# State-space mixer of a two-layer hybrid trunk: outputs formed by channel, two heads side by side in the array, and one scratch tag for two mixers' statistics

## The chip, the cores and the metric

The kernel runs on one core of a Trainium2 chip. Its engines are TensorE (PE, matrix products into PSUM; PEld is its weight load), VectorE (DVE), ScalarE (ACT), GpSimd (POOL) and SyncE (SP, which here issues DMAs). Each engine works through its own queue of instructions in order; semaphores make one wait for another. The metric is the device time of one execution in microseconds.

## The reference

Two layers, each with four token mixers (state-space SSD, RWKV-7, RG-LRU, retention) over one input projection and one output projection, and a SwiGLU feed-forward block behind them. 528 tokens (16 learned ones ahead of 512), width 1024. The mixer that the change rewrites is SSD, with 4 heads of 64 channels, 2 groups with a state of 128, in chunks of 128 tokens:

```python
def ssd_chunked(x, a, b, c):
    ...
    a_cs = jnp.cumsum(a, axis=-1)
    Lmat = jnp.exp(segsum(a))
    y_diag = jnp.einsum('bclhn,bcshn,bhcls,bcshp->bclhp', c, b, Lmat, x)
    decay_states = jnp.exp(a_cs[..., -1:] - a_cs)
    states = jnp.einsum('bclhn,bhcl,bclhp->bchpn', b, decay_states, x)
    ...
    entering = jnp.einsum('bhzc,bchpn->bzhpn', decay_chunk, states)[:, :-1]
    y_off = jnp.einsum('bclhn,bchpn,bhcl->bclhp', c, entering, jnp.exp(a_cs))
    return (y_diag + y_off).reshape(Bsz, T, H, P)
```

RWKV and retention end in a norm over each head's 64 channels, for which sums of squares by token and head are wanted (`head_group_norm`).

## The kernel before

Activations lie with channels on the partitions and tokens along the free axis, in two halves of 264 tokens. Every dense weight is streamed from DRAM as units of 128 output channels by 1024 inputs, 98 to a layer (24 of the input projection, 8 of the output projection, 44 and 22 of the feed-forward). ScalarE casts a unit to a high part and VectorE subtracts it to get the low part (L187, names `whi`, `wlo`). A unit times half the tokens is 8 k-tiles of three matmuls (L369 to L371, high by high, high by low, low by high). These are the projection matmuls. They write a PSUM bank of the pool `psb` (three banks, `pb`) or `psr` (three, `mr`); a third pool `psm` (two, `mx`) serves the mixers.

The mixers lie between the input projection and the output projection. RWKV's core (`rwkv_core`) goes through five packs p = 0 to 4, each two chunks of 64 tokens, pack 4 the tail of 16 tokens. A pack starts with transposes (L644), inverts a triangular matrix by substitution on VectorE (L675 to L684, a reduce, rounds of a shuffle with two tensor operations, and a transpose at the end), forms its results on TensorE (from L692 on, to the state's L769) and ends with `tok_stats`: ScalarE squares the pack's output into a scratch tile `gn_sq` (L448), VectorE sums it by head. Retention (`ret_core`) goes through five chunks c of 128 tokens (the last has 16) and ends each with a copy and the same `tok_stats`. SSD (`ssd_core`) goes through the same chunks; RG-LRU starts with the projection lx0, copied out of PSUM at L806.

The kernel is written in program order, in `layer`: RWKV's core and its end, then retention, then SSD's convolutions, dt and core, RG-LRU, the gates, and the ends. A scheduler then puts the instructions of all engines in an order of its own, by what they need. What bounds it are the slots of pools: a tile of a pool with k slots waits until the tile that had the slot k allocations earlier in program order is read for the last time. Two pools matter here. `up` has 16 slots of [128, 540], taken by projected tiles: retention's q, k, v and its rotation tables are among them, and hold their slots to the end of retention's chunks. `small` holds scratch tiles by tag; the scratch of `tok_stats` (L447) has one slot a tag. RWKV's calls use the tag `rw_sq` (L776), retention's `re_sq` (L1049).

In SSD's core a chunk forms `L`, the decay by pair of tokens times C·B (L887 to L894), and then token-major outputs: four matmuls with L as the weights and 64 columns each (L897), and from chunk 1 on two matmuls of C with the state, 128 columns each (L903). VectorE scales the second part by `ea`, exp of the decay's running sum, and adds the first into `ysb` (L905, L906). Two transposes turn `ysb` to channel-major (L921), and VectorE adds the skip term into `syf` (L922).

Of the kernel before, what the change touches and what calls it, by code (L numbers as in the profile page):

```python
# [14 lines left out]
ALU = mybir.AluOpType  # L15
# [29 lines left out]
# rows of the output projection, in the order in which y is held  # L45
Y_ORDER = ["rwkv0", "rwkv1", "lru0", "lru1", "ret0", "ret1", "ssd0", "ssd1"]

# [14 lines left out]
def constants():  # L62
    """Tables that depend on shapes alone."""
# [21 lines left out]
    # retention  # L85
# [26 lines left out]
def trunk(ctx, tc, hT, wstream, wdt, cols, lora, lruw, const, rope, out, dbg=None):  # L112
# [15 lines left out]
    # the identity is the first of the constants  # L128
# [13 lines left out]
    # ------------------------------------------------------------------ helpers  # L142
# [34 lines left out]
    def behind(after):  # L177
        """not to be issued ahead of the instructions given"""
        stack = ExitStack()
        for a in after:  # L180
            stack.enter_context(tc.issue_after(a.ins))
        return stack
# [6 lines left out]
    def rsqrt_small(v, n, m):  # L189
        """1/sqrt of [n, m], by Newton's steps."""  # L190
# [11 lines left out]
    def softplus_small(x, n, m):  # L202
        """log(1 + exp(x)) of [n, m]."""
# [17 lines left out]
    # ------------------------------------------------------------------ weights  # L221
    class Stream:
# [13 lines left out]
        def split(self, after=()):  # L236
            """after: instructions that it is not to be issued ahead of"""
# [26 lines left out]
    # ------------------------------------------------------------------ norms  # L264
    def rstd_bc(accs, n, keep=None, prior=None):
        """sums of squares, by partition in each of accs [128, n], -> 1/rms on every partition (in PSUM).
        keep: a place for 1/rms by token; prior: such a place, with factors that the squares still lack"""
# [25 lines left out]
    class SumSq:  # L293
        """squares of tiles, summed over the tiles"""
# [4 lines left out]
        def add(self, srcs):  # L299
            """the square of a pair of tiles"""  # L300
# [20 lines left out]
    def pair(name, n, where=None):  # L321
        """high and low part of [128, n], in one slot"""
# [12 lines left out]
    def norm_half(hs, n, wcol, ss, first=False):  # L335
        """8 tiles of h, in pairs [128, 2, n] -> the parts of rms_norm(h)"""
# [11 lines left out]
    def scaled_parts(t, n, wcol, k):  # L348
        """the parts of h * w, for one k-tile"""
# [8 lines left out]
    def load_h(src, s, n, engines=(nc.sync,), tile=pair_tile):  # L358
        """the 8 tiles of h, in pairs"""
# [5 lines left out]
    def big(ps, wt, acts, first, last):  # L365
        """ps += wt.T @ acts over the k-tiles listed"""
# [9 lines left out]
    def product(w, acts, n, i=0):  # L376
        """one unit of weights times 8 k-tiles of activations"""
# [4 lines left out]
    # ------------------------------------------------------------------ start  # L382
# [28 lines left out]
    # the table with the square root, for the squares too  # L411
# [4 lines left out]
    # derived parameters  # L416
# [957 lines left out]
```

## Time and profile before

| what | value |
|---|---|
| runs | 1520.08, 1522.01, 1521.93 us; median 1521.93 |
| the profiled execution, its span | 1520.8 us, 29707 instructions |
| TensorE busy | 1488.2 us (98%), 12654 instructions |
| VectorE busy | 805.9 us (53%) |
| ScalarE busy | 608.1 us (40%) |
| GpSimd busy | 6.0 us |
| DMA | 129.93 MB, mean 85 GB/s |

Engines overlap, so busy times don't add up to the span. A matmul's record runs from its start to a modelled end, and matmuls overlap in the array: distances between starts tell more than durations. An f32 matmul leaves two records, a transpose or a matmul of the split parts one. The granted clock (PEclk) is 1.00 at TensorE's full 2.4 GHz and 0.50 at 1.2 GHz.

### The profile page before, as it was taken

Reading aid. Unit: us, or ns where it says so; the run is one execution under the profiler, and the core shown is the slowest. Engines: PE = TensorE matmul, PEld = TensorE weight load, DVE = VectorE, ACT = ScalarE, POOL = GpSimd, SP = SyncE. Lnnn points to the kernel's source line nnn. Section 1 sums busy time; section 2 is a strip of 40 time slices with the busy share of each in tenths; the row PEclk is TensorE's granted clock in tenths of the full one; section 3 lists DMA queues with packets and bytes.
Section 4 is the critical chain, followed back from the end, with each engine's and each line's share of the span. In section 5 each row is a group of like instructions: output and inputs, shape, how many; then the busy total and the mean of one; then the engine's idle time right before and its main releaser. Section 6 shows DMA issues by size and latency. Waiting matters only on the chain.

```text
span 1520.8 us, 29707 instructions
## 1 busy us (share of the span) xinstructions
PE 1488.2 (98%) x12654; PEld 1432.1 (94%) x12654; DVE 805.9 (53%) x1961; ACT 608.1 (40%) x1132; POOL 6.0 (0%) x12
## 2 busy tenths in 40 slices
PE   7999999999999999999999999999999999999997
PEld 6998889999999999999999988899999999999997
DVE  7486656866534444322284866568665444443233
ACT  6633334756423332223255333348564233332231
POOL 0000000000000000000000000000000000000000
PEclk9999999999999999999999999999999999999998
DMA  7110100045212222222352101000551222322223
GB/s 243 64 57 29 43 29 29 29 157 166 70 56 84 84 98 97 84 93 88 112 197 63 57 29 42 29 29 30 154 179 56 70 98 85 110 84 98 98 91 104
DMA packets 50820, 129.93 MB, mean 85 GB/s; under 512 B 5120, under 2 KB 23680, under 8 KB 50560
## 3 DMA queue, kind: packets, MB, share of 16 engines
q1 hardware_dynamic: 47728, 124.22, 25.2%
q10 hardware_dynamic: 2960, 3.81, 0.8%
q8 instruction: 99, 1.62, 0.4%
q14 instruction: 33, 0.27, 0.1%
HBM read 119.50 MB, written 8.52 MB: 84 GB/s over the span
## 4 chain that ended last, share of the span: by engine, by line
PE 91%; DVE 5%; DMA 1%; ACT 1%; issue 1%; SPq 0%; DVEq 0%; ACTq 0%
PE pb L369 14%; PE pb L370 14%; PE pb L371 14%; PE mr L371 10%; PE mr L369 10%; PE mr L370 10%; PE mr L692 1%; PE mr L726 1%; PE mx L273 1%; DVE wlo L187 1%; PE mr L702 1%; PE mr L660 1%; DMA raw<-in_wstream_dram 1%; PE mr L766 1%; PE mr L756 1%
## 5 line engine op out<-in xcount | busy, mean ns | idle before, releaser
L369 PE MATMUL pb<-hn,whi 128*128 128x264 f32 (+1 forms) x1440 | 419.1, 291 | 2.4 <-ACT hn L187 2.4
L371 PE MATMUL pb<-hn,wlo 128*128 128x264 f32 (+1 forms) x1440 | 417.9, 290 | 0.0
L370 PE MATMUL pb<-hn,whi 128*128 128x264 f32 (+1 forms) x1440 | 416.5, 289 | 0.8 <-DVE hn L187 0.6
L187 DVE TENSOR_TENSOR wlo<-raw,whi 128x1024 fp32r<-128x1024 f32 x200 | 243.8, 1223 | 233.5 <-ACT whi L187 232.9
L187 ACT CAST whi<-raw 128x1024 fp32r<-128x1024 f32 x200 | 209.0, 1050 | 326.5 <-PE pb L370 131.6
L369 PEld LDWEIGHTS pb<-hn,whi 128*128 128x128 f32 x1440 | 272.7, 189 | 8.6 <-issue 3.4
L370 PEld LDWEIGHTS pb<-hn,whi 128*128 128x128 f32 x1440 | 273.3, 190 | 5.3 <-issue 2.0
L371 PEld LDWEIGHTS pb<-hn,wlo 128*128 128x128 f32 x1440 | 272.2, 189 | 3.3 <-issue 1.7
L369 PE MATMUL mr<-hn,whi 128*128 128x264 f32 (+1 forms) x800 | 228.3, 285 | 0.0
L371 PE MATMUL mr<-hn,wlo 128*128 128x264 f32 (+1 forms) x800 | 227.4, 284 | 0.1
L370 PE MATMUL mr<-hn,whi 128*128 128x264 f32 (+1 forms) x800 | 226.4, 283 | 0.0
L370 PEld LDWEIGHTS mr<-hn,whi 128*128 128x128 f32 x800 | 152.0, 190 | 0.0
L369 PEld LDWEIGHTS mr<-hn,whi 128*128 128x128 f32 x800 | 151.9, 190 | 0.0
L371 PEld LDWEIGHTS mr<-hn,wlo 128*128 128x128 f32 x800 | 150.9, 189 | 0.4 <-DVE wlo L187 0.4
L163 DVE TENSOR_TENSOR gf<-gf,mr 128x264 f32<-128x264 f32 (+1 forms) x88 | 37.4, 425 | 133.7 <-PE mr L371 130.0
L369 PE MATMUL mr<-g,whi 128*128 128x264 f32 (+1 forms) x352 | 99.9, 284 | 0.0
L370 PE MATMUL mr<-g,whi 128*128 128x264 f32 (+1 forms) x352 | 99.8, 284 | 0.0
L371 PE MATMUL mr<-g,wlo 128*128 128x264 f32 (+1 forms) x352 | 99.5, 283 | 0.0
L369 PE MATMUL pb<-g,whi 128*128 128x264 f32 (+1 forms) x352 | 99.4, 282 | 0.0
L370 PE MATMUL pb<-g,whi 128*128 128x264 f32 (+1 forms) x352 | 99.4, 282 | 0.0
L371 PE MATMUL pb<-g,wlo 128*128 128x264 f32 (+1 forms) x352 | 99.3, 282 | 0.0
L187 ACT CAST g<-gf 128x264 fp32r<-128x264 f32 (+1 forms) x88 | 35.9, 407 | 111.6 <-DVE gf L163 111.6
(397 smaller groups left out, 2406.0 us busy)
## 6 DMA issues: line engine op xcount, KB each, us to landing
raw<-in_wstream_dram SPq DMA_DIRECT2D x200, 512.0 KB, 3.5
h<-in_hT_dram SPq DMA_DIRECT2D x16, 264.0 KB, 4.5
hdram<-h SPq DMA_DIRECT2D x16, 264.0 KB, 3.0
h<-hdram SPq DMA_DIRECT2D x16, 256.0 KB, 3.9
h<-hdram SPq DMA_DIRECT2D x8, 264.0 KB, 5.3
hdram<-h SPq DMA_DIRECT2D x8, 256.0 KB, 2.2
cst<-in_const_dram SPq DMA_DIRECT2D x1, 1046.5 KB, 8.2
out_dram<-h SPq DMA_DIRECT2D x4, 256.0 KB, 2.6
```

The lines of the kernel that those rows point to most:

```text
L163: eng.tensor_tensor(out=out, in0=in0, in1=in1, op=op)
L187: last_hilo[:] = (S.copy(out=hi, in_=src), V.tensor_tensor(out=lo, in0=src, in1=hi.bitcast(F32), op=ALU.subtract))
L273: PE.matmul(pc[:m, c : c + 1], lhsT=acc[:, m * c : m * c + m], rhs=ones[:, 0:1], start=i == 0, stop=i == len(accs) - 1)
L369: PE.matmul(ps, lhsT=whi, rhs=ahi, start=first and i == 0, stop=False)
L370: PE.matmul(ps, lhsT=whi, rhs=alo, start=False, stop=False)
L371: PE.matmul(ps, lhsT=wlo, rhs=ahi, start=False, stop=last and i == m - 1)
L660: PE.matmul(pg[:, o : o + 128], lhsT=BK[rows, j, p, c, :, :], rhs=AR[rows, j, p, c, c : c + 2, :], start=True, stop=True)
L692: PE.matmul(p1[Ur[c], 32 * h : 32 * h + 32], lhsT=GM[hh][Ur[c], j, c, Ac[c]], rhs=Xt[Ur[c], h, :].rearrange("p (n two b) -> p n two b", tw ...
L702: PE.matmul(p2[Ur[c], 32 * h : 32 * h + 32], lhsT=Zt[Ur[c], h, :], rhs=T1[Ur[c], h, :], start=True, stop=True)
L726: PE.matmul(pw[Ur[c], 128 * h : 128 * h + 128], lhsT=Zt[Ur[c], h, :], rhs=RZ[Ur[c], c, h, :], start=True, stop=True)
L756: PE.matmul(py[o : o + 64, 128 * j : 128 * j + 128], lhsT=QT[:, c, j, :], rhs=St[:, j, :], start=True, stop=False)
L766: PE.matmul(pst[:, 0:128], lhsT=BT[:, c, 2 * j : 2 * j + 2, :], rhs=RZ[:, c, 2 * j : 2 * j + 2, 0:64], start=True, stop=St is None)
```

## The change

In SSD's core the outputs are formed channel-major at once. The four products of a chunk have `xdt` (128 tokens by 64 channels) as the weights and L as the moving operand of 128 columns; the two heads of a pair write partitions 0 to 63 and 64 to 127 of the same columns of one PSUM bank. From chunk 1 on the state's part is added in PSUM by four more products, with the state as the weights and `Cd` as the moving operand. `Cd` is new: exp of the decay's running sum, broadcast over the partitions (it is in PSUM as `pb`), times C. The transposes, `ysb` and `ea` are gone. Beside that, the two tags of `tok_stats`' scratch are one, `tk_sq`. The rest of the diff takes away comments.

```diff
-                tok_stats(yc[p][:nt], nt, var, p, "rw_sq")
+                tok_stats(yc[p][:nt], nt, var, p, "tk_sq")
...
-            acs, ea, dec, tot = tl("acs"), tl("eacs"), tl("sdec", 4), tl("stot", 4)
+            acs, dec, tot = tl("acs"), tl("sdec", 4), tl("stot", 4)
...
-            S.activation(out=f(ea), in_=f(acs), func=AF.Exp)
...
+                if St is not None:
+                    Cd = core("Cd", [128, 4, 128])
+                    S.activation(out=Cd[:, :, :n], in_=pb.rearrange("p (h t) -> p h t", h=4)[:, :, :n], func=AF.Exp)
+                    for g in range(2):
+                        tt(V, Cd[:, 2 * g : 2 * g + 2, :n], Cd[:, 2 * g : 2 * g + 2, :n],
+                           sd[f"C{g}"][:, tk].unsqueeze(1).to_broadcast([128, 2, n]), ALU.mult)
...
-                for h in range(4):
-                    PE.matmul(py[:n, 64 * h : 64 * h + 64], lhsT=L[:n, h, :n], rhs=xdt[:n, h, :], start=True, stop=True)
-                ysb = core("ysb", [128, 256])
-                if St is None:
-                    S.copy(out=ysb[:n], in_=py[:n, 0:256])
-                else:
-                    for g in range(2):
-                        PE.matmul(py[:n, 256 + 128 * g : 384 + 128 * g], lhsT=sd[f"C{g}"][:, tk], rhs=St[:, 2 * g : 2 * g + 2, :],
-                                  start=True, stop=True)
-                    tt(V, h4(ysb[:n]), h4(py[:n, 256:512]), sd["ea"][:n, c, :].unsqueeze(2).to_broadcast([n, 4, 64]), ALU.mult)
-                    add(V, ysb[:n], ysb[:n], py[:n, 0:256])
+                for j in range(2):
+                    for hh in range(2):
+                        PE.matmul(py[64 * hh : 64 * hh + 64, 128 * j : 128 * j + n], lhsT=xdt[:n, 2 * j + hh, :],
+                                  rhs=L[:n, 2 * j + hh, :n], start=j == 0, stop=St is None, skip_group_check=True)
+                if St is not None:
+                    for j in range(2):
+                        for hh in range(2):
+                            PE.matmul(py[64 * hh : 64 * hh + 64, 128 * j : 128 * j + n], lhsT=St[:, 2 * j + hh, :],
+                                      rhs=Cd[:, 2 * j + hh, :n], start=False, stop=True, skip_group_check=True)
+                for j in range(2):
+                    stt(V, yf[j][:, tk], sd[f"x{j}"][:, tk], Pl("s_d", j, j + 1), py[:, 128 * j : 128 * j + n], ALU.mult, ALU.add)
...
-                pt2 = mx()
-                for j in range(2):
-                    PE.transpose(pt2[:, 128 * j : 128 * j + n], ysb[:n, 128 * j : 128 * j + 128], ident[:n, :n])
-                    stt(V, yf[j][:, tk], sd[f"x{j}"][:, tk], Pl("s_d", j, j + 1), pt2[:, 128 * j : 128 * j + n], ALU.mult, ALU.add)
...
-                tok_stats(py[:n, 0:256], n, var, c, "re_sq")
+                tok_stats(py[:n, 0:256], n, var, c, "tk_sq")
```

The instructions also stand in another order. The first place is ScalarE's queue in layer 0, where the squares of `tok_stats` stand. The numbers in the names tell tiles apart: gn_sq_2304, 2333, 2362 are retention's chunks 0, 1, 2, and gn_sq_1331 is RWKV's pack 0. Before:

```order
L1048 COPY yc_2279<-mx_2292 128x256
L448 ACTIVATE gn_sq_2304<-mx_2292 128x256
L649 COPY RZ_1344<-mr_1334 128x8x64
L448 ACTIVATE gn_sq_1331<-yc_1127 128x256
L651 COPY BT_1345<-mr_1335 128x512
L1024 COPY vt_2311<-mx_2307 128x256
L1048 COPY yc_2279<-mx_2319 128x256
L448 ACTIVATE gn_sq_2333<-mx_2319 128x256
```

and now, where gn_sq_2076 is RWKV's pack 4 (16 tokens):

```order
L730 COPY Wt_2054<-mr_2049 64x256
L732 COPY RZ_1986<-mr_2049 64x4x64
L448 ACTIVATE gn_sq_2076<-yc_1127 16x256
L448 ACTIVATE gn_sq_2304<-mx_2292 128x256
L448 ACTIVATE gn_sq_2333<-mx_2319 128x256
L1026 COPY vt_2340<-mx_2336 128x256
L1050 COPY yc_2279<-mx_2348 128x256
L448 ACTIVATE gn_sq_2362<-mx_2348 128x256
```

Retention's chunk 0 stood ahead of RWKV's pack 0; now it stands behind pack 4, the last of RWKV.

The second place is ScalarE's queue where lx0 is copied out of its projection bank. Before, ahead of pack 3's substitution (its copy into Z at L676):

```order
L806 COPY C1p_2745<-pb_2779 128x264
L809 ACTIVATE C1c_2805<-C1p_2745,cols_98 128x528
L816 ACTIVATE C1c_2805<-C1c_2805 128x528
L676 COPY Z_350_2004<-cst 64x32
L206 ACTIVATE sp_2869<-dt_2859 128x20
L806 COPY lx0p_3143<-pb_3151 128x264
L207 ACT_TABLE_LOAD
```

and now, where gn_sq_2412 is retention's last chunk:

```order
L448 ACTIVATE gn_sq_2391<-mx_2377 128x256
L1026 COPY vt_2397<-mx_2394 16x256
L1050 COPY yc_2279<-mx_2405 16x256
L448 ACTIVATE gn_sq_2412<-mx_2405 16x256
L806 COPY lx0p_3136<-pb_3144 128x264
L806 COPY lx0p_3136<-pb_3170 128x264
L809 ACTIVATE lx0c_3196<-lx0p_3136,cols_98 128x528
```

The copy of lx0 has moved from about the start of pack 4 to behind retention's last chunk.

The third place is TensorE's queue in retention's chunks 1 and 2. Before, projection matmuls (L369 to L371) stand between the chunks' steps:

```order
L1034 MATMUL mx_2319<-R_2301,rqc_2263 128x256
L1036 MATMUL mx_2319<-vt_2311,sc_2317 128x64 x4
L1042 MATMUL mx_2327<-vt_2311,kd_2325 128x256
L370 MATMUL pb_2449<-hn_386,whi_2146 128x264
L371 MATMUL pb_2449<-hn_386,wlo_2147 128x264
L369 MATMUL pb_2449<-hn_390,whi_2146 128x264
L1020 MATMUL mx_2336<-cst,rv_378_2145 128x128
L1020 MATMUL mx_2336<-cst,rv_384_2204 128x128
L1022 MATMUL mx_2336<-ident,rk_2272 128x128
L1029 MATMUL mx_2344<-qx_2342,rk_2272 128x512
L370 MATMUL pb_2449<-hn_390,whi_2146 128x264
```

and now, behind pack 4's last matmul (L759):

```order
L759 MATMUL mr_2065<-RZ_1986,GM_346_1997 64x64
L1044 MATMUL mx_2327<-vt_2311,kd_2325 128x256
L1022 MATMUL mx_2336<-cst,rv_378_2145 128x128
L1022 MATMUL mx_2336<-cst,rv_384_2204 128x128
L1024 MATMUL mx_2336<-ident,rk_2272 128x128
L1031 MATMUL mx_2344<-qx_2342,rk_2272 128x512
L1036 MATMUL mx_2348<-R_2329,rqc_2263 128x256
L1038 MATMUL mx_2348<-vt_2340,sc_2346 128x64 x4
L1044 MATMUL mx_2356<-vt_2340,kd_2354 128x256
L791 MATMUL mr_2100<-ident,yc_1127 128x128
```

From pack 3's results to SSD's dt there is no projection matmul among TensorE's instructions now: a row of 205 in each layer. The longest such rows before are of 78, 52 and 34.

## Rows read from the trace of the kernel before

**Rows 1.** The page's first part: engine, busy us (share of span) x instructions.

```profile
span 1520.8 us, 29707 instructions
...
PE 1488.2 (98%) x12654; PEld 1432.1 (94%) x12654; DVE 805.9 (53%) x1961; ACT 608.1 (40%) x1132; POOL 6.0 (0%) x12
```

**Rows 2.** The page's chain that ended last, shares of the span by engine.

```profile
PE 91%; DVE 5%; DMA 1%; ACT 1%; issue 1%; SPq 0%; DVEq 0%; ACTq 0%
```

**Rows 3.** Timeline of TensorE, pack starts and ends: start us, us, engine, line, operation.

```profile
202.69 0.27 PE L644 MATMUL mr<-ident,AR 128*128 128x128 f32 x1
...
219.73 0.29 PE L369 MATMUL pb<-hn,whi 128*128 128x264 f32 x1
219.85 0.29 PE L370 MATMUL pb<-hn,whi 128*128 128x264 f32 x1
220.07 0.24 PE L692 MATMUL mr<-Xt,GM 64*64 64x32 f32 x1
...
243.02 0.27 PE L644 MATMUL mr<-ident,AR 128*128 128x128 f32 x1
...
317.71 0.28 PE L369 MATMUL pb<-y,whi 128*128 128x264 f32 x1
...
964.55 0.27 PE L644 MATMUL mr<-ident,AR 128*128 128x128 f32 x1
...
1076.61 0.28 PE L369 MATMUL pb<-y,whi 128*128 128x256 f32 x1
```

**Rows 4.** Windows: bounds, us, busy (records) of PE PEld DVE ACT POOL, PEclk, DMA share, GB/s.

```profile
268.00:317.70 49.70, 49.56 (x381) 46.65 (x381) 42.83 (x127) 37.67 (x61) 1.35 (x2) 1.00 0.18 54
...
981.90:1001.90 20.00, 20.00 (x231) 17.49 (x231) 8.12 (x35) 4.82 (x14) 0.00 (x0) 1.00 0.01 2
220.00:243.00 23.00, 23.00 (x231) 20.05 (x230) 8.16 (x35) 4.82 (x14) 0.00 (x0) 0.85 0.01 1
```

**Rows 5.** Timeline of VectorE, in pack 3's and pack 4's substitution.

```profile
212.12 0.19 DVE L679 STREAM_SHUFFLE B<-Z 128x32 f32<-128x32 f32 x1
...
212.81 0.19 DVE L679 STREAM_SHUFFLE B<-Z 128x32 f32<-128x32 f32 x1
...
210.18 0.77 DVE L160 SCALAR_TENSOR_TENSOR C0c<-C0p,cols,C0c 128x528 f32<-128x528 f32 x1
...
216.30 0.41 DVE L831 COPY dtraw<-mx 8x264 f32<-8x264 f32 x1
...
246.19 0.66 DVE L675 TENSOR_REDUCE A<-Zt 64x32 f32<-64x256 f32 x1
...
258.16 0.44 DVE L684 STREAM_TRANSPOSE Xt<-Zt 64x256 f32<-64x256 f32 x1
```

**Rows 6.** ScalarE's timeline: squares of retention's chunks 1 and 4, RWKV's pack 4.

```profile
131.51 0.39 ACT L448 ACTIVATE gn_sq<-mx 128x256 f32<-128x256 f32 x1
...
145.08 0.37 ACT L448 ACTIVATE gn_sq<-mx 16x256 f32<-16x256 f32 x1
...
267.95 0.41 ACT L448 ACTIVATE gn_sq<-yc 16x256 f32<-16x256 f32 x1
```

**Rows 7.** Windows of low granted clock, columns as in rows 4.

```profile
234.40:241.20 6.80, 6.80 (x40) 5.89 (x38) 1.79 (x5) 0.00 (x0) 0.00 (x0) 0.50 0.01 2
...
795.00:800.00 5.00, 3.86 (x28) 3.59 (x28) 3.59 (x12) 2.18 (x7) 0.00 (x0) 0.76 0.09 30
800.00:805.00 5.00, 5.00 (x27) 5.00 (x26) 3.60 (x11) 2.02 (x5) 0.00 (x0) 0.56 0.01 3
```

**Rows 8.** TensorE's timeline; then instructions with ns min/median/max, first and last start.

```profile
75.23 1.13 PE L586 MATMUL mr<-ident,kk_n 88*64 88x88 f32 x24
...
253.53 1.11 PE L882 MATMUL mx<-cst,dta 128*128 128x128 f32 x8
...
L891 ACT ACTIVATE L<-L x10: 255/616/636, 248.1 to 1055.7; 128x512 f32<-128x512 f32 x8, 16x64 f32<-16x64 f32 x2
...
L163 DVE TENSOR_TENSOR ysb<-mx,eacs x8: 413/424/426, 262.2 to 1059.3; 128x256 f32<-128x256 f32 x6, 16x256 f32<-16x256 f32 x2
```

More of the change, by code (lines that the diff above doesn't have):

```diff
@@ L856, in ssd_dt @@
             V.tensor_copy(f(acs)[0:16, 16:20], pa[0:16, 16:20])
-            S.activation(out=f(ea), in_=f(acs), func=AF.Exp)
             S.activation(out=f(dec), in_=pa[:, 32:48], func=AF.Exp)
             S.activation(out=f(tot), in_=pa[:, 64:80], func=AF.Exp)
-            sd.update(dt=dt, dta=dta, acs=acs, ea=ea, dec=dec, tot=tot)
+            sd.update(dt=dt, dta=dta, acs=acs, dec=dec, tot=tot)
         def ssd_core(cp):
```

## Prediction

> **What bounds the kernel now.** The page's first part is read first: TensorE is busy in 1488.2 of 1520.8 us, VectorE in 53% and ScalarE in 40% of the span [rows 1]. Then the chain that ended last: 91% of it is TensorE's, 5% VectorE's, 1% ScalarE's [rows 2]. Third, the stretch windows round the mixers: in 268 to 317.7, where SSD, RG-LRU and the gates are worked out, TensorE is busy for 49.56 of 49.70 us, VectorE for 42.83 and ScalarE for 37.67 [rows 4]. So the kernel holds the bound by one thing: while the mixers' chains of small steps run, projection matmuls stand between them in TensorE's queue. What an edit saves on VectorE or ScalarE counts only where a chain is late; what takes the projections out from between the chains counts in full.
>
> **The change, part by part.** All prices are per layer (there are two), from layer 0 unless said.
>
> *SSD's arithmetic on TensorE.* Removed per chunk: four matmuls of 64 columns, two of 128 by the state, two transposes. Added: four of 128 columns, and four more by the state. An f32 matmul is two records and a transpose one. If both heads of a pair run side by side in the column halves, 128 columns cost about what 64 cost; if not, twice that. The nearest row for "side by side" is L586, whose products go in turn to the two column halves: 24 records of 88 columns end within 1.13 us, 47 ns each. The nearest row for "not" is L882: 8 records of 128 columns in 1.11 us, some 120 ns up to the next instruction [rows 8]. Over the layer's five chunks, after has 40 and 32 records in the place of 40, 16 and 10. With pairs side by side I count -2.1 us, one after another +3.5 us. In the emitted order the two heads of a pair stand next to each other, as in L586, but they change weights every time. I take 0 and keep both ends.
>
> The Trainium skill, *TensorEngine Tiling (Array Packing)*, Key Properties, says that different tiles can load and multiply in parallel, but that a change of the tiling mode drains the array. L586's 47 ns agrees with the first half; no row here separates the second, which would speak against this change, since every chunk goes into half-width products and out again. By that sentence alone the term would stand at -2.1 plus the drains, which no row prices.
>
> *SSD's arithmetic elsewhere.* Four exponentials 128x512 come in, like L891's 0.62 us each, and eight products 128x256 of VectorE like those into ysb, 0.42 each; eight into ysb, one copy and one small exponential go [rows 8]. That is +2.5 us of ScalarE and about nothing on VectorE, and the Cd step stands beside L's chain, not in it. It lies under TensorE's work in a stretch where ScalarE has 12 of 49.7 us free [rows 4]; I cost it at nothing. Without that cover it is 2.5 us.
>
> *The scratch of the squares.* This decides the forecast. RWKV's and retention's statistics had a slot each; now they share one, and a slot is given out in the order in which the program is written: RWKV's five packs first. Before, retention's squares of chunks 1 to 4 ran from 131.51 to 145.45, amid the packs, and the last RWKV square came at 267.95 [rows 6]. After, as the order shows, ScalarE squares pack 3, pack 4, and only then retention's chunks 0, 1, 2, 3, 4. Until they are through, retention keeps its q, k, v and the rotation tables in the pool of 16 slots. RG-LRU's first projection, lx0, can't be evacuated until one of those is free, the three projection banks fill up, and TensorE has no projection to put between the chains: 205 small matmuls stand in a row in each layer, from pack 3's results to SSD's dt, and SSD's chunks, which used to fill this stretch, come behind it.
>
> I add up the stretch from pack 3's start to the first output-projection matmul. Before it is 202.69 to 317.71, 115.0, and 964.55 to 1076.61, 112.1 [rows 3]; mean 113.6. The work ahead of pack 3 is equal to about 1.3 us by the order; I take it as equal. After:
> (a) From pack 3's start to its results' first matmul: 17.4 now, 202.69 to 220.07 [rows 3]. Three convolution steps of 0.77 and two copies of 0.41 that are mixed in [rows 5] have moved ahead of it: 3.1 less, 14.3. The 72 projection matmuls there, 0.122 apart [rows 3], are 8.8 and fit inside.
> (b) The rest of pack 3: 231 records took 20.0 at full clock in layer 1 [rows 4]. Its 25 projection matmuls (3 us) are gone, but they lay mostly in waits; I take 0.9 off: 19.0.
> (c) Pack 4, 243.02 to its square at 267.95: 24.9 [rows 3, 6]. Its substitution, 246.19 to 258.16, is stretched by SSD's steps on VectorE; alone, a round takes 0.69 (212.12 to 212.81) [rows 5], six 4.1, and with the steps at both ends 5.6 in place of 12.0. Another 1.1 of such waits goes: 17.4.
> (d) Two squares, 0.41 and 0.39 [rows 6]: 0.8.
> (e) Retention's chunks 2 to 4: from chunk 1's square to the end of chunk 4's 13.9 now [rows 6]; 0.5 for chunk 1's late start, 1.2 off for projections between them: 13.2.
> (f) The slot comes free, lx0 is copied, a bank with it: 2.5, an estimate from copies of 0.4 and two hand-overs.
> Sum of the chain to the first projection: 14.3 + 19.0 + 17.4 + 0.8 + 13.2 + 2.5 = 67.2.
> (g) What is left for TensorE then: 312 projection matmuls and some 203 small records, 515 in all. In 268 to 317.7 it got through 381 in 49.7, 0.130 each [rows 4]: 67.0. ScalarE and VectorE have about 60 us of work of their own in it.
> Sum 134.2 against 113.6: +20.6 at full clock.
> (h) The clock. In 234.4 to 241.2 the granted clock was 0.50 (1.2 GHz) for 6.8 us [rows 7], in that very stretch of pack 3, and layer 0's 231 records took 23.0 there where layer 1's took 20.0 [rows 4]: 3.0 for one such drop. The other drop, in 800 to 805, followed on 5 us in which TensorE was busy for only 3.86 [rows 7]. The bare stretch (b) to (f) is 53 us of such work. I take two drops, +6; the bounds are none and the whole stretch and its end at 1.2 GHz, 0.44 a microsecond, +25 to +32.
> Per layer 26.6, for two layers 53.2: 1520.8 + 53.2 = 1574.0. The median of the runs stands 1.1 above the profiled span: **1575**.
>
> **The rivals.**
> *The clock stays low.* For it: PE idles most in the bare stretch, and both drops came in stretches like it. Against: pack 3's rest in layer 1 held 1.00 all through [rows 4]. Then 1520.8 + 2 x (20.6 + 25 to 32) = 1612 to 1626. The Trainium skill, *TensorE: Matmul & The Clock Gate*, on HAM oscillation, says that idle stretches between bursts take TensorE back to half its clock time and again; the two drops agree that far, and by that rule this rival is the likelier.
> *Full clock and a shorter chain.* No drop: 1521 + 41.2 + 1 = 1563; with pairs side by side, and the chain 5 us shorter since VectorE and ScalarE have little else to do: 1548.
> *The bare stretch costs nothing (the other side).* Its 52.9 us of (b) to (f) would have to shrink to 113.6 - 14.3 - 67.0 = 32.3 for TensorE's own work to fill it: the packs' chain, uncontested, would run at 60% of today's time. Then only the SSD term counts: 1522 - 4.2 = 1518 to 1522. The 0.69 of a free round speaks for some of it; against it, layer 1's 20.0 for pack 3's rest, where VectorE is busy for 8.12 only [rows 4], so that contention isn't what makes it long.
>
> **How the numbers follow.** Forecast 60%, clock low 18%, full clock 17%, the other side 5%. Range 1545 to 1620: from the shortest chain into the lower half of the low clock's times; the other half and the other side, 14%, stay outside. About 3 us (0.2%) can be told from no change; the other side's 5% is split, so faster 0.02, same 0.03, slower 0.95.
>
> **What would show it.** Right: in the trace of after, squares of retention's chunk 0 directly behind pack 4's, some 53 us of each layer without a projection matmul, TensorE's busy share of the whole near 95%, ScalarE waiting at lx0's copy for a slot, the pairs of L904 at 50 or at 120 ns a record. The stretch from pack 3 to the first output projection should read about 140, and 125 at the least. Wrong: if projections go on beside pack 4; if TensorE's granted clock is 0.5 for most of the bare stretch; or if the stretch reads under 116.

## The result, and the profile after

The changed kernel takes 1587.53 us (median of 4 runs, 1585.26 to 1589.43) against 1521.97 us for the kernel before, run beside it (1520.08 to 1525.24): a ratio of 1.0421, interval 1.0399 to 1.0444 (the ratios here are taken over all the runs of both kernels, and can differ a little from the quotient of two medians). It is slower by 65 us. The forecast was 1575 with a range of 1545 to 1620. From run to run the time of one kernel moves with TensorE's granted clock: the kernel before took from 1518.2 us at a mean of 0.995 to 1541.4 at 0.978.

The first part of the page and its chain by engine, where [rows 1, 2] had 1488.2 us of TensorE in 1520.8 and 91%. The rows of 40 slices are TensorE's busy tenths and its granted clock:

```profile
span 1584.5 us, 29778 instructions
...
PE 1511.0 (95%) x12666; PEld 1443.0 (91%) x12666; DVE 813.7 (51%) x1961; ACT 620.7 (39%) x1144; POOL 6.7 (0%) x12
...
PE   7999986999999999999999999869999999999997
...
PEclk9999977999999999999999999679999999999998
...
PE 87%; DVE 7%; ACT 2%; DMA 2%; issue 1%; SPq 0%; DVEq 0%; ACTq 0%
```

The loss sits in two places, some two of the 40 slices in each layer, where TensorE is less busy and its clock is lower at the same time. ScalarE's squares there, in layer 0 (start us, us, engine, line; in brackets how long the engine sat idle, and for whom):

```profile
259.02 0.42 ACT L448 ACTIVATE gn_sq<-yc 16x256 f32<-16x256 f32 x1 [4.02 <-DVE yc L163]
...
259.91 0.39 ACT L448 ACTIVATE gn_sq<-mx 128x256 f32<-128x256 f32 x1 [0.47 <-DVE var L449]
...
260.88 0.38 ACT L448 ACTIVATE gn_sq<-mx 128x256 f32<-128x256 f32 x1 [0.58 <-DVE var L449]
...
266.72 0.39 ACT L448 ACTIVATE gn_sq<-mx 128x256 f32<-128x256 f32 x1
...
276.46 0.39 ACT L448 ACTIVATE gn_sq<-mx 128x256 f32<-128x256 f32 x1
...
279.48 0.37 ACT L448 ACTIVATE gn_sq<-mx 16x256 f32<-16x256 f32 x1
279.75 0.62 ACT L806 COPY lx0p<-pb 128x264 f32<-128x264 f32 x2
```

The first square is RWKV's pack 4, the five behind it are retention's chunks. In [rows 6] chunk 4 was squared at 145.08; now it is at 279.48, and lx0 leaves its bank right behind it. TensorE's last projection matmul ahead of this is at 211.02, the next at 283.25: 72.2 us without one, and 72.0 in layer 1. What lies around this stretch in TensorE's timeline, with the first products of pack 3's results (L692) and the matmuls of SSD's dt (L830):

```profile
211.02 0.28 PE L371 MATMUL pb<-hn,wlo 128*128 128x264 f32 x1
214.29 1.49 PE L692 MATMUL mr<-Xt,GM 64*64 64x32 f32 x16 [2.98 <-DVE Xt L684]
...
279.10 4.00 PE L830 MATMUL mx<-hn,wdt 128*8 128x264 f32 x32
...
283.25 0.39 PE L369 MATMUL pb<-hn,whi 128*128 128x264 f32 x1
```

The stretches of layer 0 as the prediction cut them, and layer 1's whole stretch; columns as in [rows 4], the third number from the end is the granted clock:

```profile
199.38:214.29 14.91, 11.93 (x101) 11.45 (x99) 12.89 (x43) 5.24 (x9) 0.00 (x0) 1.00 0.21 67
...
214.29:240.05 25.76, 23.39 (x192) 20.78 (x193) 5.25 (x15) 2.25 (x7) 0.00 (x0) 0.54 0.01 4
240.05:259.00 18.95, 8.35 (x64) 6.82 (x62) 9.47 (x43) 1.79 (x5) 0.00 (x0) 0.63 0.00 1
259.00:283.25 24.25, 20.20 (x109) 13.13 (x109) 17.29 (x67) 6.00 (x16) 0.00 (x0) 0.87 0.00 1
283.25:347.21 63.96, 63.62 (x517) 58.24 (x516) 47.14 (x136) 52.74 (x82) 3.25 (x4) 1.00 0.15 48
...
991.52:1139.20 147.68, 127.35 (x977) 110.28 (x976) 92.04 (x302) 68.02 (x118) 3.25 (x4) 0.85 0.09 28
```

From pack 3's start to the first output-projection matmul it is 147.8 us in layer 0 and 147.7 in layer 1, against 115.0 and 112.1 [rows 3]: +32.8 and +35.6. Ahead of pack 3 the layers are 3.3 and 2.5 us shorter (retention's chunks no longer stand there), and the last part is 1.2 longer: 32.8 + 35.6 - 3.3 - 2.5 + 1.2 = 63.8, the difference of the two spans (63.7).

### The profile page after: what moved, and what is told of

Same layout as the page of the kernel before. It is cut to its first block, busy times and chain, and to the rows that moved or that the text cites. A ratio compares the mean times of both kernels' runs of the same rounds, so it can differ in the third digit from the quotient of the medians.

```text
span 1584.5 us, 29778 instructions
## 1 busy us (share of the span) xinstructions
PE 1511.0 (95%) x12666; PEld 1443.0 (91%) x12666; DVE 813.7 (51%) x1961; ACT 620.7 (39%) x1144; POOL 6.7 (0%) x12
## 4 chain that ended last, share of the span: by engine, by line
PE 87%; DVE 7%; ACT 2%; DMA 2%; issue 1%; SPq 0%; DVEq 0%; ACTq 0%
PE pb L369 13%; PE pb L370 13%; PE pb L371 13%; PE mr L371 9%; PE mr L369 9%; PE mr L370 9%; PE mr L692 2%; PE mr L726 1%; DMA raw<-in_wstream_dram 1%; PE mr L702 1%; PE mx L273 1%; DVE wlo L187 1%; PE mr L660 1%; PE mr L756 1%; PE mr L766 1%
## 5 line engine op out<-in xcount | busy, mean ns | idle before, releaser
L369 PE MATMUL pb<-hn,whi 128*128 128x264 f32 (+1 forms) x1440 | 416.8, 290 | 5.0 <-ACT hn L351 2.6
L371 PE MATMUL pb<-hn,wlo 128*128 128x264 f32 (+1 forms) x1440 | 413.5, 287 | 0.0
L369 PEld LDWEIGHTS pb<-hn,whi 128*128 128x128 f32 x1440 | 272.1, 189 | 11.5 <-issue 3.6
L371 PEld LDWEIGHTS pb<-hn,wlo 128*128 128x128 f32 x1440 | 271.6, 189 | 1.7 <-issue 0.5
L369 PE MATMUL mr<-hn,whi 128*128 128x264 f32 (+1 forms) x800 | 227.3, 284 | 0.0
L371 PE MATMUL mr<-hn,wlo 128*128 128x264 f32 (+1 forms) x800 | 226.9, 284 | 0.1
L369 PEld LDWEIGHTS mr<-hn,whi 128*128 128x128 f32 x800 | 151.0, 189 | 0.0
L371 PEld LDWEIGHTS mr<-hn,wlo 128*128 128x128 f32 x800 | 150.4, 188 | 0.4 <-DVE wlo L187 0.4
L369 PE MATMUL mr<-g,whi 128*128 128x264 f32 (+1 forms) x352 | 100.0, 284 | 0.0
L371 PE MATMUL mr<-g,wlo 128*128 128x264 f32 (+1 forms) x352 | 99.6, 283 | 0.0
L371 PE MATMUL pb<-g,wlo 128*128 128x264 f32 (+1 forms) x352 | 99.5, 283 | 0.0
L369 PE MATMUL pb<-g,whi 128*128 128x264 f32 (+1 forms) x352 | 99.4, 282 | 0.0
```

Source lines behind the costliest of these rows:

```text
L369: PE.matmul(ps, lhsT=whi, rhs=ahi, start=first and i == 0, stop=False)
L371: PE.matmul(ps, lhsT=wlo, rhs=ahi, start=False, stop=last and i == m - 1)
```

## The experiments

Eleven kernels were run. The kernel before ran beside each group; its median was 1524.65 beside the first four, 1525.34 beside the next four, 1526.68 beside the last three, so ratios are compared. Where a time is given "in the scale of 1522", it is the ratio times 1522 us. Three dots in the code stand for lines that are not shown.

### The two halves of the change

*The kernel before with one tag.*

```diff
-                tok_stats(yc[p][:nt], nt, var, p, "rw_sq")
+                tok_stats(yc[p][:nt], nt, var, p, "tk_sq")
...
-                tok_stats(py[:n, 0:256], n, var, c, "re_sq")
+                tok_stats(py[:n, 0:256], n, var, c, "tk_sq")
```

> The kernel before with one edit: both mixers' squares under one tag. Theory: the whole loss appears without any new SSD arithmetic, 1587 to 1594 us, with some 72 us per layer without a projection matmul and squares of retention directly behind pack 4's. Rival (the loss needs Cd and the new products): 1522 to 1555.

Measured: 1584.64 us, ratio 1.0402 (1.0345 to 1.0460). The longest stretches without a projection matmul are 71.8 and 72.5 us. The same cut as above, in layer 0:

```profile
198.14:213.07 14.93, 11.93 (x101) 11.46 (x99) 12.91 (x43) 5.24 (x9) 0.00 (x0) 0.97 0.20 70
213.07:238.47 25.40, 23.03 (x192) 20.42 (x193) 5.25 (x15) 2.25 (x7) 0.00 (x0) 0.55 0.01 2
238.47:257.44 18.97, 8.35 (x64) 6.83 (x62) 9.47 (x43) 1.79 (x6) 0.00 (x0) 0.62 0.00 1
257.44:281.60 24.16, 20.08 (x109) 13.06 (x109) 17.29 (x67) 5.99 (x16) 0.00 (x0) 0.88 0.00 1
281.60:345.94 64.34, 63.97 (x509) 60.55 (x508) 47.40 (x133) 52.39 (x81) 2.85 (x4) 1.00 0.15 50
```

Stretch by stretch this is the changed kernel, without a line of SSD touched. The shared tag alone gives 1.040 of the 1.042. The absolute time lies 2 us under the lower end that was expected.

*The changed kernel with two tags.* Room for the second scratch comes from giving Cd the slot of a dead tile of the same size:

```diff
-                    Cd = core("Cd", [128, 4, 128])
+                    Cd = cp.tile([128, 4, 128], F32, tag="re_qx", name=nm("Cd"), bufs=1)
...
-                tok_stats(py[:n, 0:256], n, var, c, "tk_sq")
+                tok_stats(py[:n, 0:256], n, var, c, "re_sq")
```

> The changed kernel with two tags again: RWKV's squares in tk_sq, retention's in re_sq. The room for it comes from Cd, which takes the slot of retention's qx (dead by then). Theory (the shared scratch costs everything, SSD's new arithmetic is a small gain): retention's squares come back amid RWKV's packs, projections stand beside packs 3 and 4 again, and the time is 1516 to 1521 us, 1 to 5 below the kernel before. Rival (SSD's new form costs a good part, by Cd's chain or by draining the array): 1535 to 1580.

Measured: 1534.67 us against 1524.65, ratio 1.0071 (1.0035 to 1.0108). Retention's squares are back at 117.9 to 145.0, and the bare stretch is gone. But it is not faster than the kernel before, as the theory had it, and its median lies 0.3 us under the rival's range: the form without the shared tag costs some 0.7%. In the scale of 1522 that is 1533 (the interval is 1527 to 1538), 12 us above the expected end. Of the 11.7 us by which the two profiled spans differ (1532.5 for 1520.8), 11.0 lie in the two stretches from pack 3's start to the output projection (119.8 and 118.3 us for 115.0 and 112.1). Where it goes is seen late in layer 1 (windows as before, then TensorE's timeline):

```profile
1011.32:1070.00 58.68, 58.68 (x484) 52.04 (x483) 45.14 (x165) 37.92 (x55) 2.38 (x3) 1.00 0.11 37
1070.00:1080.00 10.00, 7.14 (x42) 5.76 (x41) 7.57 (x15) 9.90 (x15) 0.00 (x0) 0.88 0.15 52
1080.00:1089.86 9.86, 9.86 (x66) 9.86 (x66) 8.48 (x18) 7.91 (x19) 0.00 (x0) 0.77 0.30 106
```

```profile
1074.43 0.33 PE L1063 MATMUL mr<-ident,yc 128*128 128x128 f32 x1 [0.55 <-DVE rg L160]
1076.98 0.39 PE L369 MATMUL pb<-hn,whi 128*128 128x264 f32 x1 [2.22 <-ACT rg L477]
```

In 1070 to 1080 ScalarE is busy for 9.90 of 10 us, and TensorE waits for it (the copy of a gate at L477), 2.9 us in all; right behind, from 1077.6, the granted clock is 0.50 for 6.8 us. The same in layer 0 at 313.0. Over the stretch from pack 3 to the first output projection ScalarE's instructions add up to 74.0 us where the kernel before has 66.7. Of these 7.3, 1.9 are Cd's exponentials and 5.1 are four more table loads of 1.28 (19 in place of 15): ScalarE's instructions stand in another order, and functions of different tables alternate more often. (The kernel before with one tag has 19 in this stretch as well, without the new form.)

### What of SSD's new form costs

*Cd without its exponentials.*

```diff
...
-                    S.activation(out=Cd[:, :, :n], in_=pb.rearrange("p (h t) -> p h t", h=4)[:, :, :n], func=AF.Exp)
...
-                        tt(V, Cd[:, 2 * g : 2 * g + 2, :n], Cd[:, 2 * g : 2 * g + 2, :n],
+                        tt(V, Cd[:, 2 * g : 2 * g + 2, :n], pb.rearrange("p (h t) -> p h t", h=4)[:, 2 * g : 2 * g + 2, :n],
```

> The kernel with two tags, but Cd is C times the running sum itself, straight from PSUM: the four exponentials of Cd a layer are left out (so SSD's state part is not the reference's). Its order keeps the 59 table loads that the kernel with two tags has (before: 51). Theory (that kernel's loss of 0.7% comes of ScalarE's table loads, 5.1 us a layer, more than of Cd's exponentials, 1.9): only a part comes back, 1525 to 1532 us in the scale of a kernel before of 1522. Rival (Cd's exponentials are the loss): at or below the kernel before, 1515 to 1522.

Measured: 1532.63 us against 1525.34, ratio 1.0035 (0.9996 to 1.0074), 1527 in the scale of 1522: in the theory's range. The table loads are still 19 in the stretch, and in layer 1 TensorE's wait at the gates falls from 2.9 to 1.8 us, with no drop of the clock behind it. The interval reaches from no loss at all to that of the kernel with two tags, so the shares of the two are not settled by this run.

*The kernel before with Cd's exponentials, unread.*

```diff
+                if St is not None:
+                    Cd = cp.tile([128, 4, 128], F32, tag="re_qx", name=nm("Cd"), bufs=1)
+                    S.activation(out=Cd[:, :, :n], in_=pb.rearrange("p (h t) -> p h t", h=4)[:, :, :n], func=AF.Exp)
```

> The kernel before, with the four exponentials 128x512 of Cd a layer added behind L's, their results unread; its order keeps 51 table loads. Theory (what costs with two tags is exponentials and table loads together, 7.2 us; 2.4 alone lie in ScalarE's free 12): ratio 0.999 to 1.003. Rival (the exponentials alone): 1.004 to 1.008.

Measured: 1524.64 us against 1526.68, ratio 0.9989 (0.9956 to 1.0021). Four exponentials a layer alone cost nothing that can be measured; the windows of layer 1, from pack 4's start on, show ScalarE with time to spare (38.59 of 50.63) and TensorE waiting for 0.3 us:

```profile
1000.30:1024.70 24.40, 24.40 (x220) 22.92 (x219) 19.91 (x75) 13.38 (x24) 1.84 (x3) 1.00 0.14 44
1024.70:1075.33 50.63, 50.33 (x386) 47.09 (x385) 42.75 (x127) 38.59 (x63) 1.07 (x1) 1.00 0.17 53
```

So the prediction's "12 of 49.7 us free" holds for the exponentials. This kernel also has Cd in the dead slot, so in that order the slot costs nothing either. That it takes the exponentials and the table loads of the other order together to make ScalarE late fits these two runs, but it is not shown: the run without the exponentials could also be a loss of 0.7%, and no run has the table loads without the new products.

*Two ways to have fewer table loads or exponentials.* The first transposes `ea` with its columns broadcast in place of the exponentials; the second takes the output bank from another pool. Both stand on the kernel with two tags.

```diff
+                    pe = mx()
+                    for h in range(4):
+                        PE.transpose(pe[:, 128 * h : 128 * h + n], sd["ea"][:n, c, h : h + 1].to_broadcast([n, 128]), ident[:n, :n])
...
```

> The kernel with two tags, but Cd's factor comes without its own exponentials: ea, one small exp a layer, is transposed with its columns broadcast (four transposes a chunk, 0.08 to 0.11 us each, 1.6 us a layer on TensorE), and VectorE multiplies it by C out of PSUM. 57 table loads in the order. Theory (with two tags the loss is ScalarE, late at RG-LRU's and the gates' end): that wait goes as it did without the exponentials, and TensorE has -1.4 + 1.6 us a layer: ratio 0.999 to 1.005 to the kernel before. Rival (the new products themselves cost): 1.006 to 1.012.

```diff
-                py = mx()
+                py = mxr()
                 for j in range(2):
                     for hh in range(2):
...
```

> The kernel with two tags, with SSD's output bank taken from the three banks psr in place of the two of psm. The order has 55 table loads (59 with py in psm, 51 before), Cd's exponentials stay. Theory (ScalarE's sum in the mixers' last stretch decides, 7.2 us more a layer with 59): 2 to 3 us a layer less on ScalarE, ratio 0.999 to 1.005. Rival (the exponentials alone decide, or py's place): as with two tags, 1.007, or above.

Measured: 1556.02 us, ratio 1.0164 (1.0105 to 1.0223), and 1562.70, 1.0249 (1.0193 to 1.0306), against 1526.68. Both miss what was expected, on the slow side. The first has 79.8 us from the first projection in pack 4 to the output projection, where the kernel before has 72.3; that each chunk now asks for one more bank of the two of psm is a candidate; it also lost much of layer 1 ahead of pack 3 to the lower clock (51 us at 0.50 there). In the second the stretch from pack 3 to the output projection is shorter than in any other kernel (107.0 and 108.5 us), but TensorE then goes 8.4 us without a projection behind the first output-projection matmul, and what follows is some 25 us longer in each layer (672.2 for 646.8, 468.5 for 444.2): work was put off, not saved. ScalarE shows it: its instructions in the shorter stretch add up to 50.5 us with 11 table loads, where the kernel before has 66.7 and 15. Neither cause was separated further. No version was found that beats the kernel before.

*Retention's squares in another dead slot.*

```diff
-                tok_stats(py[:n, 0:256], n, var, c, "tk_sq")
+                sq = core("vt", [128, 256])
+                S.activation(out=sq[:n], in_=py[:n, 0:256], func=AF.Square)
+                V.tensor_reduce(out=var[:n, c, :], in_=sq[:n].rearrange("p (h e) -> p h e", h=4), axis=AX.X, op=ALU.add)
```

> The changed kernel, but retention squares into the slot of its own vt (dead after the chunk's products) and takes no part in tk_sq. Cd keeps a slot of its own. Theory: like the kernel with two tags, 1516 to 1523 us; a chunk's vt may now wait for the sum of the chunk before, which I price at 0 to 2 us per layer. Rival (Cd or the products cost): 1535 to 1580.

Measured: 1552.69 us, ratio 1.0153 (1.0104 to 1.0203), in the rival's range and not in the theory's. This takes the shared tag away as well, and with it the bare stretch, but it costs 18 us more than two tags do by the medians (0.8% by the ratios). From pack 2's start to pack 3's it shows 44.11 us at a mean granted clock of 0.69, in both layers; in the kernel with two tags the same packs are 39.8 and 36.9 apart. A chunk's values now wait for the sum of the chunk before, which makes a chain as long as retention; that this is what brings the clock down was not tried by itself.

### The chain from the tag to the projections

*lx0's input in a place of its own*, outside the 16 slots (Cd again in the dead slot, one tag).

```diff
-            xp = U(name + "p", w=T + 3)
+            xp = cp.tile([128, T + 3], F32, tag="lx0p", name=nm(name + "p")) if name == "lx0" else U(name + "p", w=T + 3)
...
```

> The changed kernel with one tag, but lx0's padded input has a place of its own outside the pool of 16 slots (Cd sits in retention's qx slot to make room). Theory (lx0's copy waits for a slot that retention holds, and that stops the projections): lx0 is copied early, the order's bare row shrinks from 205 to 141 matmuls, one unit of 48 projection matmuls (5.9 us) moves into the bare stretch of each layer, and the clock drops later: 1560 to 1577 us. Rival (projections stop for another reason, or PE has no loss there): 1584 to 1590, no change.

Measured: 1579.02 us, ratio 1.0345 (1.0297 to 1.0393), which is 1567 to 1582 in the scale of 1522, and under the changed kernel's 1.0399 to 1.0444. The stretch without a projection is 50.3 and 53.8 us in place of 72, and what TensorE has to do behind it 60.0 in place of 64.0. So the slot does hold lx0, and lx0 holds the projections behind it, as far as this run reaches: one unit more goes through, then they stop again. The gain is at the low end of what was expected, or under it, since the clock didn't keep: in pack 3's rest the mean granted clock was 0.79 in layer 0 and 0.56 in layer 1, where the same 227 and 228 records took 24.24 and 31.28 us:

```profile
213.26:237.50 24.24, 24.24 (x227) 21.46 (x228) 6.32 (x16) 3.29 (x8) 0.00 (x0) 0.79 0.07 23
...
998.96:1030.24 31.28, 31.28 (x228) 27.56 (x229) 6.36 (x16) 3.29 (x8) 0.00 (x0) 0.56 0.06 18
```

*RWKV's end written behind retention.*

```diff
-        rwkv_final()
         ret_tables()
...
         ret_core(cp)
+        rwkv_final()
```

> The changed kernel with RWKV's end (its norm and gate, L785 to L798) written behind retention's core instead of ahead of it. In the changed kernel's trace retention's chunks 2 to 4 took 18.6 us in place of the 13.2 of the prediction, and RWKV's end stands between them on VectorE and TensorE. Theory (that contention is the excess): from the square of chunk 1 to the copy of lx0 13 to 15 us, and 1576 to 1582 us. Rival (the low clock makes the excess): 18 us again, 1584 to 1590.

Measured: 1586.05 us against 1525.34, ratio 1.0377 (1.0325 to 1.0430). Both sides got a part right: in the scale of 1522 it is 1579, inside the theory's range, but its interval is not clear of the changed kernel's. ScalarE's squares of chunks 1 to 4 and lx0's copy:

```profile
260.00 0.38 ACT L448 ACTIVATE gn_sq<-mx 128x256 f32<-128x256 f32 x1 [0.58 <-DVE var L449]
...
265.77 0.39 ACT L448 ACTIVATE gn_sq<-mx 128x256 f32<-128x256 f32 x1
...
270.22 0.39 ACT L448 ACTIVATE gn_sq<-mx 128x256 f32<-128x256 f32 x1
...
273.24 0.37 ACT L448 ACTIVATE gn_sq<-mx 16x256 f32<-16x256 f32 x1
273.51 0.62 ACT L806 COPY lx0p<-pb 128x264 f32<-128x264 f32 x2
```

Chunk 1's square to chunk 4's end is 13.6 us in place of 19.0, so RWKV's end between the chunks was the excess, as the theory had it. But the first projection comes only 6.1 us later, where it came 3.4 later before: RWKV's end and dt's matmuls now stand there. The stretch as a whole gains 3.0 and 2.6 us (144.9 and 145.1). In the profiled execution the 5.6 us were lost again between the two stretches (650.1 us for 644.3), where the clock is at 0.50 for 13.7 us in four drops; the changed kernel has one, of 3.4.

*TensorE given work for its waits*, by transposes of the identity that nobody reads: first for the two substitutions, then also behind the groups of small products that follow the substitution in packs 3 and 4 (the doubling steps of the inversion and the first products with the values, four transposes each).

```diff
...
+                if p == 4:
+                    pfl = mxr()
+                    for _ in range(64):
+                        PE.transpose(pfl[:, 0:128], ident, ident)
...
+                if p == 3:
+                    pfl = mxr()
+                    with behind((xt,)):
+                        for _ in range(26):
+                            PE.transpose(pfl[:, 0:128], ident, ident)
...
```

> The changed kernel with added transposes of the identity into an unused bank: 26 ahead of pack 3's end (they take 2.9 us, as long as TensorE would wait there) and 64 during pack 4's substitution (up to 7 us of TensorE's wait). Nothing reads them. Theory (both clock drops come of TensorE's waits in the substitutions, and cost 8 to 10 us a layer): the granted clock stays at 1.00 to the end of pack 3 at least, its rest takes 19 to 21 us in place of 25.8: 1567 to 1580 us. Rival (the low clock costs little since the chains bound, or it falls anyway): 1585 to 1595.

Measured: 1588.61 us against 1525.34, ratio 1.0394 (1.0341 to 1.0446): no gain clear of noise. TensorE's wait in pack 4's substitution fell from 7.24 to 0.24 us. The wait ahead of pack 3's results was not filled. TensorE's timeline in layer 1 has the 26 transposes 8 us before it, ahead of the projection matmuls:

```profile
994.40 3.06 PE L693 MATMUL mr<-ident 128*128 128x128 f32 x26
997.21 0.36 PE L369 MATMUL pb<-hn,whi 128*128 128x264 f32 x1
...
1003.42 0.29 PE L371 MATMUL pb<-hn,wlo 128*128 128x264 f32 x1
1005.46 0.88 PE L701 MATMUL mr<-Xt,GM 64*64 64x32 f32 x16 [1.76 <-DVE Xt L688]
```

The wait is 1.76 us in place of 2.98 since the results come 13.9 us after the pack's start in place of 14.9. The order changed as well: 21 projection matmuls that stood ahead of pack 3's results now stand behind the first of them. With these, pack 3's rest took 29.6 and 28.1 us, and the clock fell in it all the same; in layer 1 it was at 0.50 from 1007.9 on. So this run did not test its theory for pack 3.

```diff
...
+                    if p >= 3:
+                        for _ in range(4):
+                            PE.transpose(p1[:, 256:384], ident, ident)
...
```

> As the one with the waits of the substitutions filled, and four more transposes of the identity behind each group of products in the rest of packs 3 and 4 (12 groups of pack 3 to 4, about 0.3 us each at full clock, partly in TensorE's waits). Theory: the clock holds at 1.00 through packs 3 and 4, pack 3's rest takes 20 to 22 us and pack 4 some 18: 1565 to 1580. Rival: the fill only lengthens the chain: 1590 to 1600.

Measured: 1579.88 us, ratio 1.0350 (1.0293 to 1.0407). Layer 1, cut as above:

```profile
1000.50:1014.42 13.92, 12.16 (x106) 11.69 (x104) 11.86 (x42) 4.56 (x9) 0.00 (x0) 1.00 0.11 39
1014.42:1036.70 22.28, 21.21 (x241) 18.22 (x242) 6.35 (x16) 2.82 (x8) 0.00 (x0) 1.00 0.08 24
1036.70:1054.83 18.13, 14.52 (x140) 12.65 (x138) 9.50 (x43) 1.79 (x6) 0.00 (x0) 0.99 0.01 2
1054.83:1079.14 24.31, 20.29 (x109) 13.19 (x109) 17.30 (x67) 6.01 (x16) 0.00 (x0) 0.87 0.00 1
```

Here the clock held through packs 3 and 4, but for one drop of 3.4 us in layer 0. Pack 3's rest takes 22.28 us with 28 transposes and the 21 projection matmuls in it, 25.7 in the changed kernel without either; pack 4 takes 18.1 in place of 19.0. The kernel to compare with is the one with the substitutions alone filled, since its projection matmuls stand in the same places: its stretches from pack 3's start to the output projection are 150.1 and 148.8 us, here they are 144.1 and 142.6. So the lower clock costs 6 us a layer at the least, the price of the added transposes not counted. The gain in the whole time is less sure: the interval of the ratio overlaps the changed kernel's, and the profiled execution is the longest of its four runs (1590.25 us; the others took 1578.68 to 1580.70), with 27.3 us at 0.50 in layer 0 ahead of pack 3.

## Why the prediction was right

It forecast a loss of 53 us from one cause, the order that the shared tag sets, and 65 were measured. That cause is shown from both sides: the tag alone gives 1.0402, everything but the tag 1.0071. The order came as forecast: chunk 0's square directly behind pack 4's, TensorE at 95% of the whole, a long stretch without a projection.

That the number came so near is in part luck. One of the prediction's own signs of being wrong did appear: the granted clock was 0.50 for 44.4 of the 69.0 us from (b) to (f), which is most of the bare stretch. Terms that were too small and terms that were too large offset each other, and a lower clock cheaper than the prediction's price kept the sum in range. Two other signs read otherwise than forecast: the bare stretch is 72 us, not 53, and ScalarE does not sit waiting at lx0's copy, which runs straight behind chunk 4's square in its queue. By the prediction's own steps, per layer:

| step | forecast, us | measured, layers 0 and 1 |
|---|---|---|
| work ahead of pack 3, change | 0 | -3.3, -2.5 |
| (a) to pack 3's results | 14.3 | 14.9, 14.9 |
| (b) pack 3's rest | 19.0, clock apart | 25.8, 25.7 |
| (c) pack 4 to its square | 17.4 | 19.0, 19.0 |
| (d) to (f) to the first projection | 16.5 | 24.2, 24.2 |
| (g) from there to the output projection | 67.0 | 64.0, 64.0 |
| (h) clock | +6 | in (b) to (f) |
| sum, pack 3 to the output projection | 140.2 | 147.8, 147.7 |

- (a) and (c) hold. Pack 4 without SSD's steps took 18.1 at nearly full clock (0.99) in the filled kernel, 0.7 over the estimate.
- (e) is the term that was sized worst. The prediction took retention's chunks 2 to 4 at 13.2, from [rows 6], and they took 19.0. It had not seen that RWKV's end becomes ready at the same moment, pack 4's square, and stands in VectorE's and TensorE's queues between the chunks. With RWKV's end moved they took 13.6, near the predicted price. The two rows that show RWKV's end in TensorE's queue, between chunk 2's square at 266.72 and chunk 3's at 276.46:

```profile
269.38 0.33 PE L791 MATMUL mr<-ident,yc 128*128 128x128 f32 x1 [0.26 <-DVE yc L163]
...
271.99 1.50 PE L797 MATMUL mr<-glat,lora 128*128 128x264 f32 x6
```

- (d) and (f) are each about 1 us longer: 1.9 for 0.8 and 3.4 for 2.5. For (f) the prediction named lx0's copy and two hand-overs; TensorE's queue has 4.0 us of dt's matmuls there (279.10), ahead of the first projection.
- (h) has two errors that cancel, and that is luck. Two drops of 6.8 us were taken; the clock was at 0.50 for 44.4 us of each stretch, as in the rival "the clock stays low". But that rival's price, 0.44 a microsecond from [rows 4, 7], is too high there: (b) was 5.7 us longer than the chain of the kernel before at full clock [rows 4], which had 25 projection matmuls more, for 23.7 us at 0.50, some 0.24 each; pack 4's part was 0.9 longer than in the filled kernel for 14.1 us at 0.50. TensorE is busy for only 8.35 of 18.95 us in pack 4, so a slower TensorE counts for little there. Hence the rival's mechanism came in with some 7 us a layer in (b) and (c), not 25; the filled kernels bound it at 6 or more.
- What (h) read from the two drops of the kernel before was not quite what the rows show. The drop in pack 3 came while TensorE was busy for 23.00 of 23.00 us [rows 4], so not in an idle stretch. And the other did not follow on the 5 us with TensorE busy for 3.86: a mean of 0.76 over 795 to 800 [rows 7] means that the clock was at 0.50 for 2.4 of those 5 us already.
- (g): 517 records in 64.0 us, 0.124 each, in place of 515 at 0.130. The count was right.
- SSD's arithmetic on TensorE, taken at 0 between -2.1 and +3.5. In TensorE's timeline of the changed kernel four records of 128 columns, and then eight, take 0.37 and 0.58 us to the next start, 92 and 73 ns each, between the 50 and the 120 that the prediction named:

```profile
312.25 0.44 PE L904 MATMUL mx<-L,xdt 128*64 128x128 f32 x4
312.62 0.39 PE L369 MATMUL pb<-hn,whi 128*128 128x264 f32 x1
...
313.73 0.66 PE L909 MATMUL mx<-Cd,S 128*64 128x128 f32 x8
314.31 0.49 PE L916 MATMUL mx<-xdd,Bt 128*128 128x128 f32 x2
```

  By starts, from each record to the next on the engine, the removed products take 6.8 us a layer in the kernel before and the new ones 5.3: -1.4, nearer to the end for pairs. Full-width f32 records of 128 columns start 112 ns apart in the median (L882 and L910 of the kernel before), so the pairs overlap in part; fully side by side they are not seen to be. The Trainium skill, *TensorEngine Tiling (Array Packing)*, Key Properties, says that tiles of the array work in parallel: the trace agrees as far as that part. If the drains at a change of mode that it names are in these starts, they left 1.4 us of gain; no run here shows them apart.
- "I cost it at nothing", on ScalarE: right for Cd's exponentials (0.9989), wrong for the form as a whole with two tags (1.0071), where TensorE waits for ScalarE and the order has four more table loads a layer; which part of it is the loads was not separated. In the changed kernel ScalarE is busy for 52.7 of 64.0 us in the last stretch, and no loss from it shows there.
- The rival "the bare stretch costs nothing" needed the chain (b) to (f) in 32 us. It took 69.

## What to carry to other kernels

A scratch tile's tag is an order: here two users that share one slot ran in the order in which the program is written, and what waits for the second user (here the 16 slots, then lx0's copy, then the projections on TensorE) is found by following the order, not the tile's own cost of 0.4 us. When room is needed for a new tile, look for a slot that is dead at that time in program order before two scratches are put together: with Cd in the slot of retention's qx, retention's squares stayed at 117.9 to 145.0. Not every dead slot is free: vt's cost 1.0153. Where work is cut from a full engine, also count what the new order does to the others' table loads.

## What the runs showed of the hardware

The lower clock stayed in a way that the prediction did not expect. In the changed kernel TensorE was busy for 23.39 of 25.76 us in pack 3's rest, at a mean granted clock of 0.54. In the kernel before the same products, with projections between them, ran at 1.00 in layer 1 and with one drop of 6.8 us in layer 0 [rows 4].

What TensorE did ahead of a drop differs. In the changed kernel the clock fell at 214.2, at the end of a wait of 2.98 us. In the kernel with the substitutions filled it fell at 212.6 in layer 0, just behind a wait of 1.74 us, although 21 projection matmuls stood between the products that followed. With four more transposes behind each group, and a wait of the same length ahead, it held through packs 3 and 4 of layer 1, and fell for 3.4 us in layer 0. In the kernel before it fell at 234.4 with no wait of over 0.1 us in TensorE's records (their ends are modelled) since 216.77, 2.5 us behind the last projection matmul, amid small products. The Trainium skill, *TensorE: Matmul & The Clock Gate*, on HAM oscillation, has idle stretches between bursts as the cause: the waits at 214.29 and 212.29 agree with that, the drop at 234.4 shows no such idle stretch. What keeps the clock down once it has fallen was not tried apart from that.

A difference of 0.5% needed a dozen runs of each kernel here, and in the run without Cd's exponentials even that did not settle it.
